# Splitting the first weights of a decoder trunk gate by gate, and loading x on one queue

## The chip, the core and the metric

The kernel runs on one core of a Trainium2 chip. The metric is the device time of one execution in microseconds. A core has a matrix engine (PE, with its weight loader PEld), a vector engine (DVE), a scalar engine (ACT), GpSimd (POOL) and a queue engine (SP) that here only issues loads and stores. Each engine works through its own list of instructions in order and waits on semaphores for the others. PE adds into PSUM accumulators; the other engines work on SBUF and read PSUM.

## The reference

A trunk of two layers over 256 tokens of width 1024, with float32 input and output. Each layer is a SwiGLU half-step, an attention (dilated windows in the first layer, selected blocks in the second) and another SwiGLU half-step. Cut to what the change touches, the first half-step:

```python
def rmsnorm(x, g):
    xf = x.astype(jnp.float32)
    y = xf * lax.rsqrt(jnp.mean(xf * xf, axis=-1, keepdims=True) + RMS_EPS)
    return (y * g.astype(jnp.float32)).astype(x.dtype)

def swiglu(h, w_gate, w_up, w_down):
    return (jax.nn.silu(h @ w_gate) * (h @ w_up)) @ w_down
```

with `w_gate` and `w_up` of 1024 x 2816. There are four such half-steps in the kernel; two in each layer, ahead of its attention and behind it.

## The kernel before

x is held transposed: 1024 features in eight blocks of 128 rows ("row blocks", k = 0 to 7), 256 tokens each, in one SBUF tile with the norms' gains, `gains_hT`. The 2816 features of an FFN are 22 blocks of 128 ("feature blocks", f). A gate or up sum of a feature block is a product over the eight row blocks of weights.

Products keep float32's accuracy by splitting each operand into a high part, which PE can take, and a low part, the rest. For weights ACT makes the high (`wh`, a copy with rounding) and DVE the low (`wl`, the difference). For x `parts_of` does the same with the gain as factor (L100 on ACT, L98 on DVE). `products_t` then runs, for a list of accumulators, first high weights against both parts of x (L201, 512 columns wide), for all accumulators, and then low weights against x's high (L207, 256 columns wide). Lists of `sums` give the order of the accumulators.

The norm's division by the root mean square is applied later, to the finished sums; `two_squares(k)` makes the squares of the row blocks k and k + 1 on ACT (L249) and adds them up on DVE.

The first FFN opens with `opening()`: its first four feature blocks, eight sums in eight PSUM accumulators, are computed row block by row block, so that PE can begin with the first 128 rows of weights. For each k it loads 512 columns of gate and 512 of up (the tile `raw`, gate and up side by side), calls `first(k)`, which loads x two row blocks at a time on SP and scales them, then `split`, which makes highs and lows, and then `step`, which emits PE's products. k = 0 is cut in two: columns 0 to 255 (feature blocks 0 and 1), whose weights ACT's own DMA queue loads at the program's start (L118 to L120), and columns 256 to 511 (feature blocks 2 and 3), which SP loads (L541). `split(raw, 0, slice(0, S), 1)` makes gate's and up's highs of the first half apart (`by=1`); the second half has one high over both (`by=2`) and each call has one low over both. x's row block 0 comes first on SP's queue, row block 1 third on ACT's queue (L121, `load_x`). `split` ends the step's work of ACT and DVE; `two_squares` follows from k = 4 on.

After the last row block `early_joined` copies and adds the two halves of each accumulator (ACT L414, DVE L415), which gives accumulators back to the feature blocks behind.

Who comes first on an engine is decided by a scheduler that takes instructions by priority and by a model of when their operands are ready; the order of the code is the priority. `queued(p)` holds the instructions emitted under it behind the instruction stored in `marks[p]`; this sets the order of issue and adds no wait. Behind the opening, `unit` loads and splits weights 1024 columns at a time (L169, L178, L179), and the down weights come as `right` and `made` pieces (L639, L667).

Of the kernel before, what the change touches and what calls it, by code (L numbers as in the profile page):

```python
# [10 lines left out]
F32 = mybir.dt.float32  # L11
F32R = mybir.dt.float32r
AF = mybir.ActivationFunctionType
# [3 lines left out]
S = 256  # L17
NT = S // P
D = 1024
KD = D // P  # L20
# [48 lines left out]
def trunk(ctx: ExitStack, tc: tile.TileContext, a: dict, out: bass.AP):  # L69
    nc = tc.nc  # L70
# [13 lines left out]
    def atile(shape, dt=F32, name="a"):  # L84
        return ap_.tile(shape, dt, tag="a", name=name)
# [7 lines left out]
    def parts_of(hi, lo, src, scale=1.0, later=None):  # L93

        def rest():
            if isinstance(scale, float):
                return first, nc.vector.tensor_sub(lo, src, hi.bitcast(F32))  # L97
            return first, nc.vector.scalar_tensor_tensor(lo, src, scale, hi.bitcast(F32), op0=ALU.mult, op1=ALU.subtract)  # L98

        first = nc.scalar.activation(hi, src, AF.Copy, scale=scale)  # L100
        (later or (lambda call: call()))(rest)
        return first
# [9 lines left out]
    gT, hT = both[:, :GX], both[:, GX:].rearrange("p (k s) -> p k s", s=S)  # L112

    def load_x(engine, k, end):
        cols = slice(GX + k * S if k else 0, GX + end * S)
        engine.dma_start(both[:, cols], a["gains_xT"][:, cols])

    early = rawp.tile([P, 2, 2, 512], F32, tag="raw", name="raw_0")  # L118
    for i, n in enumerate(("gate", "up")):
        nc.scalar.dma_start(early[:, 0, i, :S], a[f"ffn1_w_{n}"][0][:P, :S])  # L120
    load_x(nc.scalar, 1, 2)  # L121
    BF16 = mybir.dt.bfloat16
    fill = nc.const_aps.tensor(1.0, [P, 512], BF16)
    busy = trt("busy")
# [30 lines left out]
    marks, loads = {}, []  # L155

    def queued(p):

        stack = ExitStack()
        for ins in marks.get(p, ()):  # L160
            stack.enter_context(tc.issue_after(ins.ins))
        return stack
# [33 lines left out]
    def products_t(acs, wss, xs, first, last, between=None):  # L196


        for ac, ws in zip(acs, wss):
            for i, ((wh, wl), x) in enumerate(zip(ws, xs)):  # L200
                nc.tensor.matmul(ac, wh, flat(x), start=first and i == 0, stop=False)  # L201
            if between is not None:
                between()
                between = None
        for ac, ws in zip(acs, wss):
            for i, ((wh, wl), x) in enumerate(zip(ws, xs)):
                nc.tensor.matmul(ac[:, :S], wl, x[:, 0, :], start=False, stop=last and i == len(ws) - 1)  # L207
# [4 lines left out]
    def gain(k, gi, name, tag="x"):  # L212
        if tag == "x":
            if k % 2 == 0:
                twos[name] = xp.tile([P, 2, 2, S], F32R, tag=f"xx{k // 2}", name=f"x_{name}_{k}")
            x = twos[name][:, k % 2]
        else:
            x = xp.tile([P, 2, S], F32R, tag=f"{tag}{k}", name=f"x_{name}_{k}")
        g = gT[:, gi * KD + k:gi * KD + k + 1]
        parts_of(x[:, 0, :], x[:, 1, :], hT[:, k, :], g)  # L220
        return x

    def by_token(xs):
# [3 lines left out]
    class Norm:  # L227
# [11 lines left out]
        def scale(self, k):  # L239
            self.x.append(gain(k, self.gi, self.name))  # L240
# [5 lines left out]
        def two_squares(self, k):  # L246

            sq = atile([P, 2, S], name=f"sq_{self.name}_{k}")
            nc.scalar.activation(sq, hT[:, k:k + 2, :], AF.Square)  # L249
            if k:  # L250
                nc.vector.tensor_add(self.two, self.two, sq)
            else:
                self.two = sq
            if k == KD - 2:
                self.ss = sp.tile([P, S], F32, tag="ss", name=f"ss_{self.name}", bufs=1)
                nc.vector.tensor_add(self.ss, self.two[:, 0], self.two[:, 1])
# [173 lines left out]
    def ffn_blocks(name, wg, wu, norm, first=None, beside=(), sums=None, queue=()):  # L430
# [80 lines left out]
        def early_joined(f, acs):  # L511
            return (f, *acs, *[joined(ac, f"{name}_{n}{f}", atile([P, 2, S], name=f"j_{name}_{n}{f}")[:, 0])
                               for n, ac in zip("gu", acs)])

        def opening():

            acs = [[(trt if 2 * i + j < 3 else acc)(f"{name}_{n}{i}") for j, n in enumerate("gu")] for i in range(4)]
            parts = []

            def split(raw, k, cols=slice(0, 512), by=2):  # L520
                wh, wl = parts[k]
                for i in range(0, 2, by):
                    nc.scalar.activation(wh[:, i:i + by, cols], raw[:, i:i + by, cols], AF.Copy)
                nc.vector.tensor_sub(wl[:, :, cols], raw[:, :, cols], wh[:, :, cols].bitcast(F32))

            def step(fs, *ks):
                sums = [(i, n) for i in fs for n in range(2)]
                wss = [[(wh[:, n, i * P:(i + 1) * P], wl[:, n, i * P:(i + 1) * P]) for wh, wl in parts[ks[0]:ks[-1] + 1]]
                       for i, n in sums]
                products_t([acs[i][n] for i, n in sums], wss, norm.x[ks[0]:ks[-1] + 1], ks[0] == 0, ks[-1] == KD - 1,  # L530
                           norm.gather if fs[0] == 3 else None)

            for k in range(KD):
                if k % 2 == 0:
                    raws = rawp.tile([P, 2, 2, 512], F32, tag="raw", name=f"raw_{k}") if k else early
                raw = raws[:, k % 2]
                parts.append([wp.tile([P, 2, 512], F32R, tag=tag, name=f"{tag}_0_{k}") for tag in ("wh", "wl")])
                first(k)
                if k == 0:
                    for i, w in enumerate((wg, wu)):  # L540
                        nc.sync.dma_start(raw[:, i, S:], w[:P, S:512])  # L541
                    split(raw, 0, slice(0, S), 1)
                    split(raw, 0, slice(S, 512))
                else:
                    for i, w in enumerate((wg, wu)):
                        nc.sync.dma_start(raw[:, i], w[k * P:(k + 1) * P, :512])
                    split(raw, k, by=1 if k == 1 else 2)
                if k >= KD // 2:
                    norm.two_squares(2 * k - KD)
                    if k == KD - 1:  # L550
                        norm.fold()
                if k == 0:
                    step((0, 1), k)
                    step((2, 3), k)
                elif k < KD - 2:
                    step(range(4), k)
            for i in range(4):
                step((i,), KD - 2, KD - 1)
                done.append(early_joined(i, acs[i]))

        if first is not None:
            opening()
        for f in range(4 if first is not None else 0, KF, 2):
            ws = [weights(f, n) for n in "gu"]
            if f == 0:
                acs = [[(trt if i and n == "u" else acc)(f"{name}_{n}{i}") for n in "gu"] for i in range(2)]
                for k, pair in enumerate(zip(*ws)):
                    for i in range(2):
                        for ac, (wh, wl) in zip(acs[i], pair):
                            cols = slice(i * P, (i + 1) * P)  # L570
# [23 lines left out]
    def left_sums(pairs, homes):  # L594

        sums, halves = {}, []
        assert len(pairs) <= len(homes)
        for i, home in zip(pairs, homes):
            if home in ("wh", "wl"):
                parts = wp.tile([P, 2, 512], F32R, tag=home, name=f"left_{i}")  # L600
                sums[i] = (parts[:, 0], parts[:, 1])
            elif home in ("mk", "gf"):
                parts = xp.tile([P, 2, 512], F32R, tag=home, name=f"left_{i}")
                sums[i] = (parts[:, 0], parts[:, 1])
            elif home == "qk":
                if not halves:
                    both = ap_.tile([P, 2, 2, 512], F32R, tag=home, name=f"left_{i}", bufs=2)
                    halves += [both[:, 0], both[:, 1]]
                parts = halves.pop(0)
                sums[i] = (parts[:, 0], parts[:, 1])  # L610
            elif home == "pT":
                sums[i] = tuple(pp.tile([P, 512], F32R, tag=home, name=f"left_{i}_{j}") for j in range(2))
            else:
                sums[i] = tuple(xp.tile([P, 512], F32R, tag=f"{home[:2]}{int(home[2]) + j}", name=f"left_{i}_{j}")
                                for j in range(2))
        return sums
# [590 lines left out]
    def first(k):  # L1207
        if k % 2 == 0:
            load_x(nc.sync, k, k + 2 if k else 1)
        n0.scale(k)  # L1210
# [16 lines left out]
    w, n = a["a_w_qkv"][0], HG * DH  # L1227
# [42 lines left out]
    sums = left_sums(range(9), ("mk", "kx4", "kx6", "qk", "qk", "pT", "qk", "qk", "gf"))  # L1270
# [113 lines left out]
```

## Time and profile before

| | |
|---|---|
| median of three runs | 941.29 us (941.19, 941.29, 944.08) |
| the profiled execution | 941.45 us |
| its span, first to last instruction | 939.3 us |
| granted TensorE clock, mean | 0.998 |
| POOL busy | 196.8 us (21%) |
| data moved | 259.13 MB, 276 GB/s on average |

The span is what the trace covers; the remaining 2.15 us of the profiled execution lie around it. In the views below, L201 is line 201 of the kernel above, `f_g<-x_n,wh` names output and inputs, `128x512` their shape, and a bracket at a row's end is the time that the engine was idle ahead of it, with what ended that. `SPq` and `ACTq` rows are loads being issued. Buffer numbers are left out of names, so all four gate sums of the opening read `f_g`.

### The profile page before, as it was taken

The page shows a single profiled execution, that of the slowest core. Times are in us where ns is not written, and L with a number is a line of the kernel's source. Part 1 is how long each engine was busy: PE and PEld are TensorE (multiplying, and loading weights), DVE is VectorE, ACT ScalarE, POOL GpSimd, SP SyncE. Part 2 cuts the span into 40 slices and gives each one's busy share as a digit, 9 for nine tenths or more (in the row PEclk, how much of TensorE's full clock was granted, in tenths as well). Part 3 has the DMA queues.
Part 4 walks back from the last instruction along what each step waited for, and adds up shares of the span by engine and source line. Part 5 has one row for each costly group of instructions (what it writes and reads, how often), then busy time and mean ns, then how long its engine had stood idle before and what let it go on. Part 6 is the DMA issues. An engine that isn't in the chain of part 4 may idle for free.

```text
span 939.3 us, 15039 instructions
## 1 busy us (share of the span) xinstructions
PE 931.9 (99%) x5222; PEld 808.8 (86%) x5222; DVE 859.3 (91%) x1523; ACT 660.7 (70%) x1165; POOL 196.8 (21%) x211
## 2 busy tenths in 40 slices
PE   9999999999999999999999999999999999999997
PEld 7888888888899888888888888888888988888886
DVE  7999989988989999889989998899889889979887
ACT  7866667767887666667786656787587876657773
POOL 0132100024461401100024320000254623600000
PEclk9999999999999999999999999999999999999999
DMA  9999778988879999858999986799699689997791
GB/s 330 362 355 335 200 278 277 361 263 282 214 175 259 281 365 279 231 170 327 347 324 311 321 253 180 256 331 379 209 361 243 175 241 304 284 245 255 257 364 49
DMA packets 182380, 259.13 MB, mean 276 GB/s; under 512 B 28320, under 2 KB 126368, under 8 KB 178848
## 3 DMA queue, kind: packets, MB, share of 16 engines
q1 hardware_dynamic: 169504, 229.20, 73.3%
q0 software_dynamic: 12224, 28.32, 14.5%
q8 instruction: 41, 0.67, 0.3%
q10 hardware_dynamic: 576, 0.66, 0.2%
q14 instruction: 35, 0.29, 0.1%
HBM read 242.94 MB, written 48.76 MB: 311 GB/s over the span
## 4 chain that ended last, share of the span: by engine, by line
PE 99%; DMA 0%; ACT 0%; issue 0%; SPq 0%; POOLq 0%; DVE 0%; POOL 0%; ACTq 0%
PE f_g L201 17%; PE f_u L201 17%; PE f_u L207 9%; PE f_g L207 9%; PE dn_f_d L190 4%; PE dn_f_d L194 4%; PE dn_f_d L192 4%; PE dn_f_d_m L192 3%; PE dn_f_d_m L190 3%; PE dn_f_d_m L194 3%; PE ot_bo L887 1%; PE ot_ao L887 1%; PE ot_bo L888 1%; PE ot_ao L888 1%; PE ot_bo L889 1%; PE ot_ao L889 1%
## 5 line engine op out<-in xcount | busy, mean ns | idle before, releaser
L201 PE MATMUL f_g<-x_n,wh_f_g 128*128 128x512 f32 x672 | 170.4, 392 | 0.0
L201 PE MATMUL f_u<-x_n,wh_f_u 128*128 128x512 f32 x672 | 168.8, 390 | 0.0
L201 PEld LDWEIGHTS f_u<-x_n,wh_f_u 128*128 128x128 f32 x672 | 126.1, 188 | 26.6
L201 PEld LDWEIGHTS f_g<-x_n,wh_f_g 128*128 128x128 f32 x672 | 123.0, 188 | 23.7
L179 DVE TENSOR_TENSOR wl_f_u<-raw_f_u,wh_f_u 128x1024 fp32r<-128x1024 f32 x84 | 101.5, 1214 | 3.7 <-ACT wh_f_u L178 3.3
L178 ACT ACTIVATE wh_f_u<-raw_f_u 128x1024 fp32r<-128x1024 f32 x84 | 88.0, 1051 | 20.7 <-PE f_g L201 12.6
L179 DVE TENSOR_TENSOR wl_f_g<-raw_f_g,wh_f_g 128x1024 fp32r<-128x1024 f32 x84 | 101.6, 1214 | 0.8 <-ACT wh_f_g L178 0.5
L207 PE MATMUL f_u<-x_n,wl_f_u 128*128 128x256 f32 x672 | 96.7, 283 | 0.0
L207 PE MATMUL f_g<-x_n,wl_f_g 128*128 128x256 f32 x672 | 96.3, 282 | 0.0
L178 ACT ACTIVATE wh_f_g<-raw_f_g 128x1024 fp32r<-128x1024 f32 x84 | 87.0, 1051 | 11.6 <-PE f_u L201 6.4
L207 PEld LDWEIGHTS f_g<-x_n,wl_f_g 128*128 128x128 f32 x672 | 90.7, 191 | 4.0
L207 PEld LDWEIGHTS f_u<-x_n,wl_f_u 128*128 128x128 f32 x672 | 87.6, 192 | 0.0
L303 POOL TENSOR_TENSOR d_n<-w_n,expo 128x8 f32<-128x8 f32 x5 | 11.1, 2223 | 278.5 <-DVE w_n L299 278.5
L648 POOL COPY scrap<-act_f 128x1 f32<-128x1 f32 x19 | 41.3, 2176 | 129.5 <-ACT act_f L100 115.7
L677 POOL DMA_DIRECT2D made_f_d<-made_f_d x44 | 26.4, 643 | 95.4 <-DVE made_f_d L672 25.5
L100 ACT ACTIVATE left<-q_f 128x512 fp32r<-128x512 f32 x35 | 21.9, 626 | 29.8 <-DVE q_f L425 29.6
L980 POOL TENSOR_SCALAR sm_a<-sm_a,ls_a 128x128 f32<-128x128 f32 (+1 forms) x32 | 32.9, 1059 | 29.1 <-ACT sm_a L970 16.2
L480 ACT ACTIVATE g_f<-g_f 128x512 f32<-128x512 f32 x30 | 19.0, 632 | 27.9 <-DVE g_f L479 27.4
L980 POOL TENSOR_SCALAR sm_b<-sm_b,ls_b 128x128 f32<-128x128 f32 (+1 forms) x32 | 32.9, 1046 | 26.9 <-ACT sm_b L970 21.8
L97 DVE TENSOR_TENSOR left<-q_f,left 128x512 fp32r<-128x512 f32 x35 | 23.9, 683 | 14.0 <-ACT left L100 14.0
L100 ACT ACTIVATE act_f<-g_f 128x256 fp32r<-128x256 f32 x60 | 21.6, 407 | 13.3 <-DVE g_f L483 13.3
L414 ACT ACTIVATE u_f<-f_u 128x256 f32<-128x256 f32 x60 | 22.0, 384 | 12.4 <-PE f_u L207 12.3
(785 smaller groups left out, 2485.8 us busy)
## 6 DMA issues: line engine op xcount, KB each, us to landing
raw_f_g<-in_ffn_w_gate_dram SPq DMA_DIRECT2D x42, 1024.0 KB, 9.5
raw_f_u<-in_ffn_w_up_dram SPq DMA_DIRECT2D x42, 1024.0 KB, 8.1
raw_f_d<-in_ffn_w_down_dram SPq DMA_DIRECT2D x17, 1024.0 KB, 6.0
right_f_d<-in_ffn_w_down_dram SPq DMA_DIRECT2D x32, 512.0 KB, 9.9
raw_f_d<-in_ffn_w_down_dram SPq DMA_DIRECT2D x27, 512.0 KB, 4.8
made_f_d<-in_ffn_w_down_dram SPq DMA_DIRECT2D x44, 256.0 KB, 7.7
made_f_d<-made_f_d POOLq DMA_DIRECT2D x44, 256.0 KB, 6.6
right_f_d<-in_ffn_w_down_dram POOLq DMA_DIRECT2D x16, 512.0 KB, 8.6
```

The costliest lines, as they stand in the source:

```text
L97: return first, nc.vector.tensor_sub(lo, src, hi.bitcast(F32))
L100: first = nc.scalar.activation(hi, src, AF.Copy, scale=scale)
L178: nc.scalar.activation(wh, r, AF.Copy)
L179: nc.vector.tensor_sub(wl, r, wh.bitcast(F32))
L190: nc.tensor.matmul(ac, xh, wh, start=first, stop=False)
L192: nc.tensor.matmul(ac, xh, wl, start=False, stop=False)
L194: nc.tensor.matmul(ac, xl, wh, start=False, stop=last)
L201: nc.tensor.matmul(ac, wh, flat(x), start=first and i == 0, stop=False)
L207: nc.tensor.matmul(ac[:, :S], wl, x[:, 0, :], start=False, stop=last and i == len(ws) - 1)
L648: mark = nc.gpsimd.tensor_copy(scrap, latest[-1][:, 0, 0:1].bitcast(F32))
L677: nc.gpsimd.dma_start(self.home[:, j, n], part)
L980: done = nc.gpsimd.tensor_scalar(sm[:, seg], sm[:, seg], ls[:, t:t + 1], None, op0=ALU.mult)
```

## The change

Four edits, in `opening()`, the trunk's head, `gain` and `Norm.two_squares`.

- `load_x(nc.scalar, 1, 2)` goes from ACT's queue to SP's, as the fourth load there, behind the second halves of the first weights.
- `split` makes a high and a low for gate and one of each for up where `by=1`, which now holds for both halves of k = 0, for k = 1 and for k = 2; before, the low was always one over both.
- `step` lists the gate sums of its feature blocks ahead of the up sums; before they alternated.
- The first `two_squares` is emitted at k = 2, ahead of that step's split, and the others one step later; marks hold squares behind a scaled x or a high. The marks are set for every later norm too.

```diff
-    load_x(nc.scalar, 1, 2)
...
-        parts_of(x[:, 0, :], x[:, 1, :], hT[:, k, :], g)
+        marks["squares", 0 if k == 2 else -k] = [parts_of(x[:, 0, :], x[:, 1, :], hT[:, k, :], g)]
...
-            nc.scalar.activation(sq, hT[:, k:k + 2, :], AF.Square)
+            with queued(("squares", k)):
+                nc.scalar.activation(sq, hT[:, k:k + 2, :], AF.Square)
...
                 for i in range(0, 2, by):
-                    nc.scalar.activation(wh[:, i:i + by, cols], raw[:, i:i + by, cols], AF.Copy)
-                nc.vector.tensor_sub(wl[:, :, cols], raw[:, :, cols], wh[:, :, cols].bitcast(F32))
+                    own = slice(i, i + by)
+                    high = nc.scalar.activation(wh[:, own, cols], raw[:, own, cols], AF.Copy)
+                    marks["squares", 2 if k == 2 else -k] = [high]
+                    nc.vector.tensor_sub(wl[:, own, cols], raw[:, own, cols], wh[:, own, cols].bitcast(F32))
 
             def step(fs, *ks):
-                sums = [(i, n) for i in fs for n in range(2)]
+                sums = [(i, n) for n in range(2) for i in fs]
...
                         nc.sync.dma_start(raw[:, i, S:], w[:P, S:512])
+                    load_x(nc.sync, 1, 2)
                     split(raw, 0, slice(0, S), 1)
-                    split(raw, 0, slice(S, 512))
+                    split(raw, 0, slice(S, 512), 1)
                 else:
                     for i, w in enumerate((wg, wu)):
                         nc.sync.dma_start(raw[:, i], w[k * P:(k + 1) * P, :512])
-                    split(raw, k, by=1 if k == 1 else 2)
-                if k >= KD // 2:
+                    if k == 2:
+                        norm.two_squares(0)
+                    split(raw, k, by=1 if k < 3 else 2)
+                if k > KD // 2:
                     norm.two_squares(2 * k - KD)
```

ACT's first work on data, from x of row block 0 to the highs of k = 2, before (a name's last number is a buffer's; `wh_0` are highs of k = 0, `x_n_0` is x of row blocks 0 and 1):

```order
L100 ACTIVATE x_n_0_151<-gains_hT 128x256
L523 ACTIVATE wh_0_148<-raw_88 128x256 x2
L523 ACTIVATE wh_0_148<-raw_88 128x2x256
L100 ACTIVATE x_n_0_151<-gains_hT 128x256
L523 ACTIVATE wh_1_177<-raw_88 128x512 x2
L100 ACTIVATE x_n_2_206<-gains_hT 128x256 x2
L249 ACTIVATE sq_n_0_264<-gains_hT 128x512
L523 ACTIVATE wh_2_203<-raw_202 128x1024
```

and of the change:

```order
L100 ACTIVATE x_n_0_150<-gains_hT 128x256
L524 ACTIVATE wh_0_147<-raw_88 128x256 x4
L100 ACTIVATE x_n_0_150<-gains_hT 128x256
L524 ACTIVATE wh_1_180<-raw_88 128x512 x2
L100 ACTIVATE x_n_2_210<-gains_hT 128x256
L249 ACTIVATE sq_n_0_215<-gains_hT 128x512
L524 ACTIVATE wh_2_207<-raw_206 128x512
L100 ACTIVATE x_n_2_210<-gains_hT 128x256
L524 ACTIVATE wh_2_207<-raw_206 128x512
```

The wide high of k = 0 became two, that of k = 2 two with an x high between them, and the first square moved ahead of one x high.

PE's first half step (feature blocks 0 and 1 of k = 0; the accumulators are f_g and f_u of block 0, then of block 1), before:

```order
L201 MATMUL f_g_140<-x_n_0_151,wh_0_148 128x512
L201 MATMUL f_u_141<-x_n_0_151,wh_0_148 128x512
L201 MATMUL f_g_142<-x_n_0_151,wh_0_148 128x512
L201 MATMUL f_u_143<-x_n_0_151,wh_0_148 128x512
L207 MATMUL f_g_140<-x_n_0_151,wl_0_149 128x256
```

and of the change:

```order
L200 MATMUL f_g_139<-x_n_0_150,wh_0_147 128x512
L200 MATMUL f_g_141<-x_n_0_150,wh_0_147 128x512
L200 MATMUL f_u_140<-x_n_0_150,wh_0_147 128x512
L200 MATMUL f_u_142<-x_n_0_150,wh_0_147 128x512
L206 MATMUL f_g_139<-x_n_0_150,wl_0_148 128x256
```

Both gate sums now stand ahead of both up sums; every step of the opening is turned round in this way, and PE's list is otherwise as before.

ACT at the end of the opening, where the joins of feature blocks 0 and 1 meet the highs of feature blocks 4 and 5's weights, before:

```order
L178 ACTIVATE wh_f_g_0_404<-raw_f_g_402 128x1024
L178 ACTIVATE wh_f_g_4_408<-raw_f_g_402 128x1024
L414 ACTIVATE j_f_g_348<-f_g_140 128x256
L414 ACTIVATE j_f_u_351<-f_u_141 128x256
L178 ACTIVATE wh_f_u_0_414<-raw_f_u_412 128x1024
L414 ACTIVATE j_f_g_362<-f_g_142 128x256
L414 ACTIVATE j_f_u_365<-f_u_143 128x256
L178 ACTIVATE wh_f_u_4_418<-raw_f_u_412 128x1024
```

and of the change:

```order
L177 ACTIVATE wh_f_g_0_410<-raw_f_g_408 128x1024
L177 ACTIVATE wh_f_g_4_414<-raw_f_g_408 128x1024
L414 ACTIVATE j_f_g_354<-f_g_139 128x256
L414 ACTIVATE j_f_u_357<-f_u_140 128x256
L414 ACTIVATE j_f_g_368<-f_g_141 128x256
L414 ACTIVATE j_f_u_371<-f_u_142 128x256
L177 ACTIVATE wh_f_u_0_420<-raw_f_u_418 128x1024
L414 ACTIVATE j_f_g_382<-f_g_143 128x256
```

The joins of block 1 moved ahead of the first high of up's weights.

Elsewhere: SP's list has one load of up in layer 0's second FFN behind the four `made` copies that followed it, and a few neighbours of that kind exchanged in the first FFN; in the norms behind the two attentions the first square on ACT stands behind x highs, and the first highs of the weights stand behind two more x highs and a square. Nothing that is computed differs.

## Prediction

> **What bounds the kernel now.** First the page's busy times, then the waits of PE, then PE's timeline from the start.
>
> ```profile
> PE 931.9 (99%) x5222; PEld 808.8 (86%) x5222; DVE 859.3 (91%) x1523; ACT 660.7 (70%) x1165; POOL 196.8 (21%) x211
> ```
>
> PE is busy for 931.9 of 939.3 us. The list of PE's waits over the whole span has three rows (engine, line, what it waited for; total, times, longest):
>
> ```profile
> PE busy L126 <- PEq L1367: 0.8, 1, 0.8
> PE f_g L201 <- ACT wh L523: 0.4, 1, 0.4
> PE f_g L201 <- DVE x_n L98: 0.3, 1, 0.3
> ```
>
> So PE waits three times, 1.5 us in all, and the timeline puts all three before 6.70 us (start, duration, the wait in brackets):
>
> ```profile
> 4.70 0.47 PE L201 MATMUL f_g<-x_n,wh 128*128 128x512 f32 x1 [0.26 <-DVE x_n L98]
> ...
> 6.07 0.28 PE L207 MATMUL f_u<-x_n,wl 128*128 128x256 f32 x1
> 6.70 0.50 PE L201 MATMUL f_g<-x_n,wh 128*128 128x512 f32 x1 [0.35 <-ACT wh L523]
> ...
> 8.20 0.39 PE L201 MATMUL f_g<-x_n,wh 128*128 128x512 f32 x1
> 8.43 0.39 PE L201 MATMUL f_u<-x_n,wh 128*128 128x512 f32 x1
> ...
> 10.99 0.40 PE L201 MATMUL f_g<-x_n,wh 128*128 128x512 f32 x1
> ```
>
> 4.70 is the first product of row block 0 (k=0), 8.20 of k=1, 10.99 of k=2. Matmuls overlap, so starts count, not durations: 512-wide ones follow each other every 0.23 (8.20 to 8.43). A step is eight 512-wide and eight 256-wide matmuls. Step k=1 takes 10.99 − 8.20 = 2.79, step k=0 takes 8.20 − 4.70 = 3.50 for the same work. The difference, **0.71 us**, lies between its two halves: 6.07 to 6.70 is a wait for the highs of the second half's weights. That is the most this change can recover in the opening, and nothing behind it waits on PE: an edit elsewhere can only cost.
>
> **Why PE waits at 6.70.** ACT's and DVE's timelines, and the loads (issue time, time of issuing; then KB and us from issue to landing):
>
> ```profile
> 3.94 0.89 ACT L523 ACTIVATE wh<-raw 128x256 fp32r<-128x256 f32 x2
> 6.01 0.63 ACT L523 ACTIVATE wh<-raw 128x512 fp32r<-128x512 f32 x1 [1.19 <-DMA raw<-in_ffn_w_up_dram]
> 6.55 0.49 ACT L100 ACTIVATE x_n<-gains_hT 128x256 fp32r<-128x256 f32 x1
> 6.95 1.14 ACT L523 ACTIVATE wh<-raw 128x512 fp32r<-128x512 f32 x2
> ...
> 9.40 1.06 ACT L523 ACTIVATE wh<-raw 128x1024 fp32r<-128x1024 f32 x1
> ```
>
> ```profile
> 1.17 0.42 SPq L541 DMA_DIRECT2D raw<-in_ffn_w_gate_dram  x1
> 1.63 0.43 SPq L541 DMA_DIRECT2D raw<-in_ffn_w_up_dram  x1
> 1.65 0.45 ACTq L116 DMA_DIRECT2D gains_hT<-in_gains_xT_dram  x1
> 2.11 0.43 SPq L546 DMA_DIRECT2D raw<-in_ffn_w_gate_dram  x1
> 2.58 0.43 SPq L546 DMA_DIRECT2D raw<-in_ffn_w_up_dram  x1
> ...
> raw<-in_ffn_w_gate_dram SPq DMA_DIRECT2D x1, 128.0 KB, 3.0
> raw<-in_ffn_w_up_dram SPq DMA_DIRECT2D x1, 128.0 KB, 4.3
> gains_hT<-in_gains_xT_dram ACTq DMA_DIRECT2D x1, 128.0 KB, 4.5
> raw<-in_ffn_w_gate_dram SPq DMA_DIRECT2D x1, 256.0 KB, 4.5
> raw<-in_ffn_w_up_dram SPq DMA_DIRECT2D x1, 256.0 KB, 4.7
> ```
>
> The single high at 6.01 covers gate and up together. Gate's half landed at 1.17 + 3.0 = 4.2, up's at 1.63 + 4.3 = 5.9, so gate waits for up, and PE's next matmul reads gate.
>
> **The change, part by part.**
>
> *Gate and up split one by one, gate's sums first.* One 256-wide high takes:
>
> ```profile
> L523 ACT ACTIVATE wh<-raw 128x256 fp32r<-128x256 f32 x2 | 0.8, 408 | 0.1
> ```
>
> Gate's second half is then made behind the first two highs, at 3.94 + 0.89 = 4.83, and is ready at 5.24. PE wants it at 4.70 + 2.79/2 = 6.10: no wait. Up's second half starts at 6.01 as before, is ready at 6.42, and reaches PE some 0.06 later (the old high ended at 6.64, PE started at 6.70): 6.48. With the gate sums of both feature blocks ahead, up is wanted at 6.10 + 2 × 0.23 = 6.56. That holds by 0.08; beyond it PE stalls one for one. By the old order of sums it would be wanted at 6.33 and cost 0.15, so the reordering is worth having.
>
> The split costs ACT 2 × 0.41 − 0.63 = 0.19 for the second half of k=0, and as much or less for k=2 (k=1 was split already). DVE:
>
> ```profile
> 4.06 0.48 DVE L98 SCALAR_TENSOR_TENSOR x_n<-gains_hT,x_n 128x256 fp32r<-128x256 f32 x1 [3.17 <-ACT x_n L100]
> ...
> 6.68 0.69 DVE L524 TENSOR_TENSOR wl<-raw,wh 128x512 fp32r<-128x512 f32 x1 [1.13 <-ACT wh L523]
> ...
> L415 DVE TENSOR_TENSOR j_f_g<-f_g,j_f_g 128x256 f32<-128x256 f32 x4 | 1.7, 416 | 0.0
> ```
>
> A 256-wide low is not in the trace; another two-input operation of that size takes 0.42, so a split low costs about 2 × 0.42 − 0.69 = 0.14 more, four times (two in k=0, one each in k=1, k=2). The bounds are 0 and, if a 256-wide one took as long as the 512-wide, 0.69. All of this falls beside the idle 1.19 of ACT and 1.13 of DVE in the rows above; without that cover it would delay k=1 by 0.14 to 0.33.
>
> *x of the second row block on SP's queue.* It is issued at 2.11 instead of 1.65, ACT saves 0.45 of issuing, and each later SP load is issued 0.43 later, raw_1's gate at 2.58. Where x_1 lands the trace doesn't show. It landed at 1.65 + 4.5 = 6.13; in its new place the neighbour, raw_1's gate, landed at 2.11 + 4.5 = 6.64, an upper bound as that has twice the bytes. Taking those 256 KB off at the rate of the row below (0.71) gives 5.93 as the lower bound. I take 6.13, between them. Then ACT's high of x_1 follows up's, from 6.37 to 6.86, DVE's low from 6.89 to 7.37, and PE is released 0.16 later (4.06 + 0.48 = 4.54, PE at 4.70): **7.53**. Gate's high of k=1 runs 6.77 to 7.39 and reaches PE at 7.45. Back to back, k=1 would start at 4.70 + 2.79 = 7.49. So k=1 starts at about 7.5 instead of 8.20: **0.67 to 0.71** gained. The weights of k=2 are then wanted at 10.28. Their high began at 9.40 behind both x highs and, as the row shows, waited for nothing; a single one for gate (0.63) behind one x high fewer ends by 10.03.
>
> ```profile
> 3.00:4.00 1.00, 1.00 (x4) 0.30 (x3) 0.00 (x0) 0.99 (x4) 0.00 (x0) 1.00 1.08 347
> 7.00:8.00 1.00, 1.00 (x7) 0.83 (x6) 0.77 (x2) 1.00 (x4) 0.00 (x0) 1.00 1.06 371
> ```
>
> The last columns are the granted clock, DMA share and GB/s: the transfers run at 347 with two queues in use and at 371 with one. [...]
>
> *Squares moved, and what follows from it.* In the opening the square of blocks 0 and 1 goes between x_2 and its weights instead of behind both x. Later norms have their first square behind x highs and the weights' first high two places later. Those weights were ready long before use:
>
> ```profile
> 293.37 1.04 ACT L178 ACTIVATE wh_f_g<-raw_f_g 128x1024 fp32r<-128x1024 f32 x1
> ...
> 303.72 0.62 PE L201 MATMUL f_g<-x_n,wh_f_g 128*128 128x512 f32 x2
> ```
>
> Some 9 us lie between; two x highs of 0.49 and a square, like the 0.63 of another 512-wide operation of ACT, are 1.6 us. I cost this at nothing; without that cover it would be up to 1.6 at each norm.
>
> *One load of up moves behind four copies on SP* (layer 0's second FFN):
>
> ```profile
> 321.03 0.38 SPq L169 DMA_DIRECT2D raw_f_u<-in_ffn_w_up_dram  x1
> ...
> raw_f_u<-in_ffn_w_up_dram SPq DMA_DIRECT2D x1, 1024.0 KB, 10.2
> ...
> 351.81 3.79 PE L201 MATMUL f_u<-x_n,wh_f_u 128*128 128x512 f32 x16
> ```
>
> It landed at 331.2 and was used at 351.8. Four issues of 0.43 make it some 1.7 us later, more where one of them waits for its buffer. I cost this at nothing while the 20 us between, less the two highs of 1.06 and as much for the lows that split it, some 4, are not used up.
>
> *End of the opening.* What is late next:
>
> ```profile
> 24.74 1.06 ACT L178 ACTIVATE wh_f_u<-raw_f_u 128x1024 fp32r<-128x1024 f32 x1 [0.54 <-DMA raw_f_u<-in_ffn_w_up_dram]
> ...
> 27.31 0.41 DVE L415 TENSOR_TENSOR j_f_u<-f_u,j_f_u 128x256 f32<-128x256 f32 x1
> ...
> 28.00 2.00 PE L201 MATMUL f_g<-x_n,wh_f_g 128*128 128x512 f32 x8
> ```
>
> Feature block 4 writes an accumulator that this join gives back at 27.72, 0.28 ahead of PE. With PE 0.7 earlier the old order would stall by about 0.4. The new order puts both joins of block 1 ahead of the high at 24.74 that waits for its load, so they no longer stand behind that wait and its 1.06 us, and the 0.7 survives.
>
> **Sum.** The profiled execution took 941.45 (span 939.3 and 2.15 around it); less 0.70 gives 940.75. The median of the runs is 941.29, 0.16 lower, so by it 940.6. I forecast **940.7**, within 0.3% (2.8 us, about what a measurement of this kernel can tell from no change).
>
> **Rivals.** *x_1 late, gain halved:* x_1 lands at 6.64 like the load whose place it takes. Its high starts 0.08 later (as up's did), 0.49 + 0.48 + 0.16 follow, k=1 starts at 7.9: gain 0.3, 941.1. For it speaks the place in the queue, against it the bytes.
>
> *Slower, by the same load:* behind the weights x_1 decides the start of k=1, and from a landing later than about 6.95 on it starts later than 8.20. Were it to land at 2.58 + 4.7 = 7.28, k=1 would begin at 8.5 and the kernel take 941.8. Against it: that is the landing of a load with 384 KB more ahead of it or in it.
>
> *Nothing kept:* the opening gains 0.7, and a place without slack gives it back. The nearest is PE's weight loader late in the kernel:
>
> ```profile
> PEld dn_f_d_m L192 <- DVE wl_f_d_6c L739: 0.2, 1, 0.2
> ```
>
> Here DVE is just in time. But its work before that was itself released by PE, so it moves along; if not, 941.4. The same time comes out if up's load keeps PE waiting in the opening whatever the order.
>
> *A downstream stall of more than 2.8 us* from the reordered loads or splits: needs the 16 or 9 us above used up, and would give 944.3 or more.
>
> **Chances.** Forecast 0.76; x_1 late 0.11; nothing kept 0.06; slower by x_1 0.05; large stall 0.02. Range 940.2 to 941.9: below, the full 0.71 on the median (940.58) and a spread of 0.1 as between the two lower runs, with some room for x_0's high starting sooner without ACT's third issue; above, the slower rival. Faster by over 0.3% 0.01 (no 2.8 us to be had), same 0.96, slower 0.03 (the stall, or a run like the 944.08).
>
> **What would show it.** Right: k=1 starts near 7.5, PE's row of waits on ACT's highs at 6.70 is gone, block 4 starts near 27.3, and PE ends 0.7 sooner. Wrong: a wait on x_n's low ahead of k=1, a wait on up's high at 6.5, a wait at 27.3 for the joins, or any wait of PE behind 30 us.

## The result and the profile after

The change is slower: 949.48 us (median of 6 runs, 948.16 to 955.49) against 941.83 for the kernel before (6 runs, 941.19 to 944.08) on the same chip. The ratio is 1.0088 with a 95% interval of 1.0061 to 1.0114. The forecast of 940.7 and its range up to 941.9 were wrong. The profiled execution took 948.22 with a span of 946.1, so 6.8 us more span than before, at a granted clock of 0.995.

The page's busy times, after the change:

```profile
PE 935.5 (99%) x5222; PEld 811.0 (86%) x5222; DVE 859.4 (91%) x1527; ACT 659.0 (70%) x1167; POOL 191.8 (20%) x211
```

PE has the same 5222 matmuls and is busy 3.6 us longer. So about half of the 6.8 us is idle PE, and half is PE doing the same work more slowly. The waits of PE over the span (what it waited for; total, times, longest):

```profile
PE f_u L206 <- DVE wl_f_u L178: 3.8, 1, 3.8
PE busy L125 <- PEq L1372: 0.8, 1, 0.8
```

Both short waits of the opening are gone from the list, and one long wait is new: PE waits for lows of up's weights. PE's timeline shows the place; first after the change,

```profile
76.03 1.11 PE L206 MATMUL f_g<-x_n,wl_f_g 128*128 128x256 f32 x8
80.92 2.36 PE L206 MATMUL f_u<-x_n,wl_f_u 128*128 128x256 f32 x8 [3.78 <-DVE wl_f_u L178]
83.08 3.62 PE L200 MATMUL f_g<-x_n,wh_f_g 128*128 128x512 f32 x8
...
90.40 1.78 PE L200 MATMUL f_g<-x_n,wh_f_g 128*128 128x512 f32 x7
```

then the same products before:

```profile
76.18 1.11 PE L207 MATMUL f_g<-x_n,wl_f_g 128*128 128x256 f32 x8
77.14 1.12 PE L207 MATMUL f_u<-x_n,wl_f_u 128*128 128x256 f32 x8
...
83.66 2.00 PE L201 MATMUL f_g<-x_n,wh_f_g 128*128 128x512 f32 x8
```

These are feature blocks 12 to 14 of the first FFN; 83.66 is the start of block 14 before, 90.40 after. Up's lows were due 0.96 behind gate's (76.18 to 77.14), so at 76.99, and came at 80.92: **3.93 us** of standstill. From there to block 14 PE took 9.48 instead of 6.52: **2.96 us**, at half clock, as the next view shows. Less the 0.15 that PE was still ahead at 76.03, that makes 6.74: the whole loss in the span of this execution, one of the shortest of the six.

Stretches of 2 us, after the change (PE, PEld, DVE, ACT, POOL busy with counts; granted clock, DMA share, GB/s):

```profile
78.00:80.00 2.00, 0.00 (x0) 0.00 (x0) 0.69 (x2) 1.97 (x5) 0.44 (x1) 1.00 1.09 349
80.00:82.00 2.00, 1.07 (x4) 0.93 (x4) 2.00 (x3) 0.91 (x2) 1.12 (x1) 0.50 1.09 347
82.00:84.00 2.00, 2.00 (x8) 1.75 (x8) 2.00 (x6) 0.47 (x2) 0.61 (x2) 0.50 1.14 258
```

The clock stays at 0.50 until 86 us; before, it is 1.00 in all these stretches. Matmuls take nearly twice as long at 0.50 (3.62 for eight wide ones against 2.00).

**Back along the chain.** DVE and ACT, after the change:

```profile
79.31 0.43 DVE L97 TENSOR_TENSOR act_f<-act_f,act_f 128x256 fp32r<-128x256 f32 x1 [5.26 <-ACT act_f L100]
79.65 2.35 DVE L178 TENSOR_TENSOR wl_f_u<-raw_f_u,wh_f_u 128x1024 fp32r<-128x1024 f32 x2
```

```profile
67.94 1.06 ACT L177 ACTIVATE wh_f_u<-raw_f_u 128x1024 fp32r<-128x1024 f32 x1 [0.49 <-PE f_g L200]
...
76.70 1.06 ACT L177 ACTIVATE wh_f_g<-raw_f_g 128x1024 fp32r<-128x1024 f32 x1 [5.42 <-DMA raw_f_g<-in_ffn_w_gate_dram]
...
78.87 0.40 ACT L100 ACTIVATE act_f<-act_f 128x256 fp32r<-128x256 f32 x1
```

The lows that PE wants could have been made from 69 us on: their last high began at 67.94. They stand on DVE behind one low of an activation (`act_f` of block 10), which needs its high, which stands on ACT behind highs of blocks 14 and 15's gate weights, whose load has not landed. A load for a *later* pair of blocks stops PE, because three engines work their lists in order. Before, the same pair of lows began at 73.78:

```profile
73.78 2.35 DVE L179 TENSOR_TENSOR wl_f_u<-raw_f_u,wh_f_u 128x1024 fp32r<-128x1024 f32 x2
```

It ended at 76.13, only 1.0 us before PE took it up at 77.14. That was the slack of this place.

**Why the load is late.** The load with its landing time, before, then SP's own list and the transfers around it after the change (KB, us from issue to landing):

```profile
60.27 0.42 SPq L169 DMA_DIRECT2D raw_f_g<-in_ffn_w_gate_dram  x1
...
raw_f_g<-in_ffn_w_gate_dram SPq DMA_DIRECT2D x1, 1024.0 KB, 8.3
```

```profile
60.95 0.55 SPq L644 DMA_DIRECT2D right_f_d<-in_ffn_w_down_dram  x1
61.56 0.61 SPq L168 DMA_DIRECT2D raw_f_g<-in_ffn_w_gate_dram  x1
...
raw_f_g<-in_ffn_w_gate_dram SPq DMA_DIRECT2D x1, 1024.0 KB, 15.1
right_f_d<-in_ffn_w_down_dram POOLq DMA_DIRECT2D x1, 512.0 KB, 10.8
right_f_d<-in_ffn_w_down_dram SPq DMA_DIRECT2D x1, 512.0 KB, 10.5
```

The load is issued 1.3 us later but lands 8.1 us later (76.7 against 68.6). Beside it run two transfers of 512 KB into the `right` pieces of the down weights: the fourth and last copy, now issued by SP directly ahead of it (at 48.78 before, ahead of the third group of `made` loads), and the first of POOL's adding transfers, which add another part of the weights to a piece of the same tile. POOL paces those with a tiny copy that reads the newest activation:

```python
        def paced(self):
            scrap = sp.tile([P, 1], F32, tag="scrap", name="scrap")
            mark = nc.gpsimd.tensor_copy(scrap, latest[-1][:, 0, 0:1].bitcast(F32))
            with tc.issue_after(mark.ins):
                self.add()
```

POOL before, then after:

```profile
61.11 3.59 POOL L648 COPY scrap<-act_f 128x1 f32<-128x1 f32 x1 [5.04 <-ACT act_f L100]
64.65 1.16 POOL L644 DMA_DIRECT2D right_f_d<-in_ffn_w_down_dram  x1
```

```profile
59.68 0.87 POOL L653 COPY scrap<-act_f 128x1 f32<-128x1 f32 x1 [2.76 <-ACT act_f L100]
60.50 1.16 POOL L649 DMA_DIRECT2D right_f_d<-in_ffn_w_down_dram  x1
```

The pacing copy starts 1.4 us earlier and takes 2.7 less, so the adding transfer starts **4.15 us** earlier: beside the gate load instead of behind it. What released it earlier is ACT, before and after:

```profile
58.76 1.99 ACT L178 ACTIVATE wh_f_g<-raw_f_g 128x1024 fp32r<-128x1024 f32 x2
60.65 0.40 ACT L100 ACTIVATE act_f<-act_f 128x256 fp32r<-128x256 f32 x1
```

```profile
59.20 0.42 ACT L100 ACTIVATE act_f<-act_f 128x256 fp32r<-128x256 f32 x1 [0.72 <-DVE act_f L464]
...
60.05 1.04 ACT L177 ACTIVATE wh_f_g<-raw_f_g 128x1024 fp32r<-128x1024 f32 x1
```

The high of `act_f` of block 8 stands ahead of two highs of gate's weights (blocks 12 and 13) instead of behind them. Together, in 64 to 66 us, the transfers move 184 GB/s after the change against 357 before:

```profile
64.00:66.00 2.00, 2.00 (x15) 1.84 (x14) 2.00 (x4) 0.00 (x0) 0.19 (x1) 1.00 0.98 184
```

```profile
64.00:66.00 2.00, 2.00 (x14) 1.80 (x13) 2.00 (x6) 0.04 (x1) 2.00 (x3) 1.00 1.06 357
```

### The profile page after: what moved, and what is told of

Same layout as the page of the kernel before. It is cut to its first block, busy times and chain, and to the rows that moved or that the text cites. A ratio compares the mean times of both kernels' runs of the same rounds, so it can differ in the third digit from the quotient of the medians.

```text
span 946.1 us, 15060 instructions
## 1 busy us (share of the span) xinstructions
PE 935.5 (99%) x5222; PEld 811.0 (86%) x5222; DVE 859.4 (91%) x1527; ACT 659.0 (70%) x1167; POOL 191.8 (20%) x211
## 4 chain that ended last, share of the span: by engine, by line
PE 97%; DMA 2%; ACT 0%; DVE 0%; SPq 0%; issue 0%; POOLq 0%; POOL 0%
PE f_g L200 17%; PE f_u L200 16%; PE f_u L206 9%; PE f_g L206 9%; PE dn_f_d L189 4%; PE dn_f_d L191 4%; PE dn_f_d L193 4%; PE dn_f_d_m L191 3%; PE dn_f_d_m L189 3%; PE dn_f_d_m L193 3%; DMA raw_f_g<-in_ffn_w_gate_dram 2%; PE ot_ao L892 1%; PE ot_bo L892 1%; PE ot_bo L893 1%; PE ot_ao L893 1%; PE ot_ao L894 1%
## 5 line engine op out<-in xcount | busy, mean ns | idle before, releaser
L303 POOL TENSOR_TENSOR d_n<-w_n,expo 128x8 f32<-128x8 f32 x5 | 13.2, 2632 | 274.5 <-DVE w_n L299 274.4
L653 POOL COPY scrap<-act_f 128x1 f32<-128x1 f32 x19 | 36.0, 1894 | 134.6 <-ACT act_f L100 112.4
L100 ACT ACTIVATE x_n<-gains_hT 128x256 fp32r<-128x256 f32 x48 | 21.6, 498 | 12.5 <-DVE gains_hT L845 8.5
```

The costliest lines, as they stand in the source:

```text
L653: mark = nc.gpsimd.tensor_copy(scrap, latest[-1][:, 0, 0:1].bitcast(F32))
```

## The experiments

Eleven kernels, each timed against the kernel before on the same chip. Single runs of the kernel before lie between 941.1 and 948.3, so the intervals count, not single runs. Two exchanges are to be told apart: SP's fourth copy ("copy ahead" as before, "behind" as after the change) and POOL's first adding transfer ("late" at 64 to 65.5 us as before, "early" at 60 to 61).

### x alone, and the change without it

`x_alone` is the kernel before with only x of row block 1 moved:

```diff
-    load_x(nc.scalar, 1, 2)
...
                         nc.sync.dma_start(raw[:, i, S:], w[:P, S:512])
+                    load_x(nc.sync, 1, 2)
```

> Only x of the second row block is moved to SP's queue; split, sums and squares are as before. The order theory (one load more on SP's queue makes the scheduler put the fourth copy of right_f_d behind the third group of made_f_d, the gate load behind it lands some 8 us later, PE stops once for about 4 us near 77 us and then runs some 6 us at half clock) expects the same stop, and 947.5 to 949.5. The head-start theory (PE reaches the loads too early because the opening is shorter) expects no stop, since nothing in the opening is faster here: 941.0 to 942.5.

Measured: 948.79, ratio 1.0075 (1.0056 to 1.0093), adding transfer at 60.82. PE's waits:

```profile
PE f_u L206 <- DVE wl_f_u L178: 3.8, 2, 3.6
```

`x_on_act` is the change with these two lines put back.

> The whole change but for the move of x: x of the second row block stays third on ACT's queue. The order theory expects no stop of PE near 77 us, as SP's order in the first FFN is that of before, and 940.6 to 941.3; the first product of k=1 starts at 7.5 to 7.7 if what held it at 7.89 was gate's weights of k=1 landing at 7.18 behind x. The head-start theory, and a third one by which the split's own instructions cost the time, expect 947 or more.

Measured: 941.97, ratio 0.9999 (0.9988 to 1.0010), no stop in the first FFN, adding transfer at 64.34, the gate load landing 7.3 after its issue. So the loss comes with x's change of queue and is whole without the split, the order of sums or the squares. It doesn't come from where x lands: k = 1 began at 7.89 in the change and at 7.87 without x's move. It comes through what the scheduler makes of the move 50 us later.

### SP's fourth copy, from both sides

`copy_pinned` is the change with the third group of `made` loads held behind the fourth copy; only that copy changes its place.

```diff
+                if self is f10 and not self.copies:
+                    for n in range(4):
+                        tc.add_manual_dep(m10.last[2, n].ins, copy.ins.name, ...
```

> The whole change, and the fourth copy of right_f_d ahead of the third group of made_f_d on SP, as before; that one instruction of the kernel moves and no other. The order theory expects the gate load to land near 69 instead of 76.6, no stop of PE near 77 us, and 940.9 to 941.4. The head-start theory expects 947 or more.

Measured: 949.18, ratio 1.0060 (1.0041 to 1.0080). The adding transfer is still early (60.29), the gate load lands 10.8 after its issue, and the stop at 77 is gone; but another comes one pair later, behind a load of up (issued at 73.91, landing 12.8 later against 9.9 before):

```profile
PE f_g L206 <- DVE wl_f_g L178: 3.0, 1, 3.0
```

`copy_late` is the kernel before with the copy moved behind that group, and the gate load behind the copy.

```diff
...
-                with tc.issue_after(loads[-1].ins):
-                    nc.sync.dma_start(*self.copies.pop(0))
+                fourth = self is f10 and len(self.copies) == 1
+                with tc.issue_after((m10.last[2, 3] if fourth else loads[-1]).ins):
+                    copy = nc.sync.dma_start(*self.copies.pop(0))
...
```

> The kernel before, with the fourth copy of right_f_d put behind the third group of made_f_d on SP and nothing of the change. The order theory expects a stop of PE of 3 to 5 us near 77 us and 946 to 950. If the other loads that the change moved in the first FFN (one gate load ahead of the first group of made_f_d) are needed for it too: 941.3 to 943. The head-start theory: 941.3.

Measured: 942.82, ratio 1.0018 (1.0000 to 1.0037), from 941.27 to 949.78; adding transfer at 65.17. The profiled run, 947.96, is the second longest of ten and has two stops at 88.0 to 90.8:

```profile
PE f_g L209 <- DVE wl_f_g L181: 2.1, 2, 1.3
```

The theory until here, that the copy's place decides, falls: put back it saves nothing that can be told, moved alone it costs about 0.2%, at the edge of what these runs can tell.

### SP's whole order, from both sides

An SP order of the first FFN is forced by edges along a list (g, u: loads of gate and up by feature block; r: copies; m: `made` groups):

```diff
+    for one, two in zip(order, order[1:]):
+        tc.add_manual_dep(two.ins, one.ins.name, ...
```

`sp_as_before` is the change with SP's order of before, "g4 u4 g6 u6 r0 g8 u8 r1 m0 g10 u10 r2 m1 g12 u12 r3 m2 g14 u14 ...".

> The whole change, with SP's loads of the first FFN held in the order of before (the fourth gate load behind the first group of made_f_d, the fourth copy of right_f_d ahead of the third group). The theory that SP's order makes the stop expects no stop of PE behind 70 us and 940.9 to 941.8. If the other engines' order in the first FFN, which the move of x changed too, makes it, the time stays at 945 to 949.

Measured: 952.05, ratio 1.0102 (1.0061 to 1.0142): not better than the change itself, with the adding transfer at 60.79. `sp_as_after` is the kernel before with SP's order of the change, "... r1 g10 m0 u10 r2 m1 g12 u12 m2 r3 g14 ...".

> The kernel before, opening and all, with SP's loads of the first FFN held in the order of the changed kernel. The theory of SP's order expects a stop of PE of 3 to 4 us near 77 us and 946 to 950. The other engines' order, or the head start, as the cause: 941.3 to 943.

Measured: 944.66, ratio 1.0021 (1.0001 to 1.0040), with the adding transfer at 65.48 and no stop in the profiled run. So SP's list is worth about 0.2%, and the rest of the 0.9% is elsewhere.

### The adding transfer, and DVE's order

`add_later` is the change with POOL's first two adding transfers one step later:

```diff
-... [(at, f10) for at in (4, 5, 7, 8)])
+... [(at, f10) for at in (5, 6, 7, 8)])
```

> The whole change, with POOL's first two adding transfers of right_f_d one step of the first FFN later each. If the fourth copy of right_f_d and the gate load behind it are slow because they run beside POOL's adding transfer (2048-byte packets of 140 to 340 ns on both queues between 60 and 70 us, 186 GB/s in all), the gate load lands by 72 instead of 76.6 and the stop at 77 us is gone or under 1 us: 941 to 945. If only the place behind the third group of made_f_d counts, the load still lands near 76 and the time stays at 947 to 949.5.

Measured: 944.22, ratio 1.0026 (1.0001 to 1.0052), the first adding transfer at 78.06, no stop at 77, the gate load landing 10.2 after its issue. About two thirds of the loss are gone (by the interval, two fifths at least), with the change's order untouched on SP and on ACT. The single runs go from 940.92 to 950.89, and three of the ten are longer than 947.5, so the loss does not go in every run.

`lows_first` is the change with DVE's low of block 10's activation behind the two lows that PE waits for:

```diff
+            if name == "f10_u12":
+                tc.add_manual_dep(marks["low", "f10", 10].ins, low.ins.name, ...
```

> The whole change, with one instruction of DVE moved: the low of the eleventh activation block (act_f) goes behind the two up lows of the pair that PE waits for. If PE stops at 77 us because those lows stand behind that act_f, which waits for ACT, which waits for the next pair's gate load, then the stop at 77 us goes though the gate load still lands near 76.6, and the time falls to 941 to 945 (a later stop of the same kind may stay). If PE waits for the load itself: 947 to 949.5.

Measured: 950.32, ratio 1.0073 (1.0048 to 1.0097). The stop at 77 is gone though the gate load lands at 77.6, so the chain through DVE's list was read rightly. But PE then waits for what comes behind:

```profile
PE f_u L202 <- ACT wh_f_u L177: 1.5, 1, 1.5
PE f_g L208 <- DVE wl_f_g L178: 1.1, 1, 1.1
```

The transfers stay late, and another engine's list passes that on to PE.

### ACT's one high, from both sides

`high_back` is the change with the high of block 8's activation held behind the two gate highs, as before. SP's fourth copy goes back to its old place by itself, through the scheduler.

```diff
+    tc.add_manual_dep(marks["act", "f10", 8].ins, marks["wh", "f10_g12", 4].ins.name, ...
```

> The whole change, with one instruction of ACT held in its old place: the high of the ninth activation block of the first FFN (act_f) behind the two gate highs of the seventh pair instead of ahead of them. POOL's pacing copy reads that high, and POOL's first adding transfer of right_f_d follows it. The new theory (the high comes early, the copy falls where DVE is idle and takes 0.9 us instead of 3.6, the adding transfer starts at 60.5 instead of 64.6 and runs beside SP's copy of right_f_d, both slow, and the gate load behind lands late) expects the transfer at 64 to 65, the gate load by 72, no stop of PE near 77 us, and 940.9 to 942.5. If the early transfer is only a sign of something else that the move of x did: 946 to 951.

Measured: 943.25, ratio 1.0018 (1.0001 to 1.0035). POOL is back at its old pace, and the gate load lands 7.6 after its issue:

```profile
62.27 3.26 POOL L653 COPY scrap<-act_f 128x1 f32<-128x1 f32 x1 [5.33 <-ACT act_f L100]
65.47 1.16 POOL L649 DMA_DIRECT2D right_f_d<-in_ffn_w_down_dram  x1
```

`high_ahead` is the kernel before, opening and all, with that one high ahead of the two gate highs. SP's fourth copy moves behind by itself.

```diff
+    tc.add_manual_dep(marks["wh", "f10_g12", 0].ins, marks["act", "f10", 8].ins.name, ...
```

> The kernel before, opening and x as before, with that one high of ACT put ahead of the two gate highs, where the change has it. The new theory expects the adding transfer at 60 to 61.5, the gate load at 74 or later, a stop of PE near 77 us, and 946 to 951, with nothing of the change in it. Otherwise: 941.3 to 944.

Measured: 947.51, ratio 1.0066 (1.0053 to 1.0079). The gate load lands at 74.0, as the theory had it. In the profiled run, 944.91 and the shortest of the six, PE stops several times from 77 us on for 1.0 us at most, not once for 4, and the clock stays at 1.00 there. POOL's rows and PE's waits in it:

```profile
60.68 0.47 POOL L648 COPY scrap<-act_f 128x1 f32<-128x1 f32 x1 [4.16 <-ACT act_f L100]
61.09 1.16 POOL L644 DMA_DIRECT2D right_f_d<-in_ffn_w_down_dram  x1
```

```profile
PE f_u L207 <- DVE wl_f_u L179: 1.1, 3, 0.4
PE f_g L207 <- DVE wl_f_g L179: 1.0, 1, 1.0
```

This pair settles the place: one order of ACT, 17 us ahead of the stop, turns most of the loss on without any of the change's edits and off with all of them. It doesn't settle what that order does by itself, since SP's copy moves along with it. For that the table of all kernels is read by columns (medians in us):

| | copy ahead | copy behind |
|---|---|---|
| adding transfer late | before 941.8 to 942.2, `x_on_act` 942.0, `high_back` 943.3 | `copy_late` 942.8, `sp_as_after` 944.7 |
| adding transfer early | `copy_pinned` 949.2, `sp_as_before` 952.1 | change 949.5, `x_alone` 948.8, `high_ahead` 947.5, `lows_first` 950.3 |

Each kernel of the lower row is slower by its median than each of the upper, by 2.8 us where they are nearest (947.5 against 944.7); between the columns there is no such line. `add_later` (944.2), which takes the transfer out of the stretch altogether, belongs to the upper row. It is the one kernel that parts the transfer from ACT's order, which it has as the change has it (the high of block 8 at 60.03, ahead of the two gate highs). So the early adding transfer carries most of the loss. By the ratios the line is thinner: the intervals of `copy_pinned` (from 1.0041) and `add_later` (up to 1.0052) overlap.

How the early transfer reaches PE is shown for the change alone. Where PE stops, and how often, differs among the lower row's kernels, and the landing of the gate load does not sort them: it landed at 71.7 in `copy_pinned` and at 71.9 in `add_later`, whose profiled runs took 949.55 and 943.18.

### A try at a faster kernel

`act_add_later` is `x_on_act` with the adds of `add_later`.

> The change without the move of x, and POOL's first two adding transfers one step later each: a try at a faster kernel. If the stretch from 56 to 95 us keeps its slack, what the opening gains (0.3 to 0.7) is kept in every run: 940.5 to 941.3, against 941.97 for the same kernel with the transfers in their old steps. If the transfers then crowd the loads of the pairs behind: 942 to 946.

Measured: 944.53, ratio 1.0021 (1.0004 to 1.0038): no faster. Its first adding transfer starts at 72.70, so it too belongs with the upper row. The profiled run has no stop between 30 and 130 us; its waits lie in several other places, of 0.2 to 0.5 us each, one of them at the start of feature block 4 (28.09), and their cause stays open. No kernel here beat the one before.

## Why the prediction was wrong

- **"... an edit elsewhere can only cost."** True, and that cost should have been priced. The prediction named one load that moves on SP in layer 0's second FFN and gave it 20 us of cover. The exchanges in the first FFN, which the order of instructions also showed, got no price at all: SP's were named without one, and ACT's high of block 8 was not named. This is the step that failed: the row of before needed for it (lows done at 76.13, taken up at 77.14) was in the trace, with 1.0 us of slack.
- **The change's reach.** Of x's move the prediction counted the issues on SP and ACT in the opening. Its larger effect was on the scheduler's order far behind: one ACT high, through POOL's pacing copy, the start of a transfer, a load and DVE. Why the scheduler exchanges those two on ACT when x changes its queue was not traced.
- **Rival "a downstream stall of more than 2.8 us".** The right outcome ("944.3 or more"), with a chance of 0.02 and the wrong places: it needed "the 16 or 9 us above used up". Neither was touched. Nor did it hold that a stall costs more than its length; here 3.93 us cost 2.96 more through the clock.
- **Rival "nothing kept".** Its mechanism, a place without slack, was right in kind. "The nearest" was not PE's weight loader late in the kernel, and the price was not the 0.7 us gained, since more than the opening's lead had moved.
- **The opening's 0.67 to 0.71.** The mechanism holds: the waits of the opening are gone from PE's list. The size was off. k = 1 starts at 7.89, 0.31 sooner, not 0.67, and no run shows the 0.70 of the sum. PE, then the loads of x_1 and of gate's k = 1, then ACT, all after the change:

```profile
7.89 1.20 PE L200 MATMUL f_g<-x_n,wh 128*128 128x512 f32 x4
```

```profile
gains_hT<-in_gains_xT_dram SPq DMA_DIRECT2D x1, 128.0 KB, 4.4
raw<-in_ffn_w_gate_dram SPq DMA_DIRECT2D x1, 256.0 KB, 4.6
```

```profile
7.21 1.28 ACT L524 ACTIVATE wh<-raw 128x512 fp32r<-128x512 f32 x2 [0.21 <-DMA raw<-in_ffn_w_gate_dram]
```

The sum put x_1 at 6.13 and gate's high of k = 1 at 6.77, behind x_1's. x_1 landed at 2.11 + 4.4 = 6.5, so the x_1-late rival was nearer there. But gate's weights came last: issued at 2.58, as the prediction itself said, they landed at 7.18, and ACT waited for them. The sum moved their issue by 0.43 and left their landing where it was, at 6.64. They explain only the last part of the delay: PE's last product of k = 0 began at 7.55, and low products follow each other every 0.12, so about 0.2 us. `x_on_act` was expected to begin k = 1 at 7.5 to 7.7 with these weights out of the way and began it at 7.87, with no gap ahead of it; there its first two products lay 0.56 apart (4.70 to 5.26; 0.30 before), 0.49 in the change (4.53 to 5.02). Why was not traced. The lead was 0.19 at k = 2 and 0.14 at feature block 4 (27.86 against 28.00); that part was not traced further. And an opening doesn't start k = 1 at a fixed time: in the profiled runs it began between 7.74 and 8.77 with the change's opening, between 8.20 and 8.55 with that of before. A lead of 0.3 us is smaller than this scatter, and `x_on_act`, which had 0.34 at feature block 4 in its profiled run, shows none in its time (0.9999).
- **Rival "slower, by the same load".** x_1 would have had to land later than about 6.95; it landed at 6.5. The sign was right, the mechanism not.
- **The range.** Its upper end, 941.9, was set by events in the opening alone. A place with 1.0 us of slack behind loads that change their order has no such narrow bound.

## What to carry to other kernels

When a kernel's list is made by a scheduler, an edit's cost is not where the edit is: compare the order of every engine over the whole program, and for each exchange compute, from rows of before, how far ahead of its use the thing behind it was ready. A transfer that is paced by a tiny instruction starts when that instruction gets its turn, so an order of another engine decides which loads it runs beside (here it started 4.15 us sooner, beside the gate load instead of behind it). And where the bounding engine has about 1 us of slack, price a stop at its length plus what the clock does after it (here 3.93 and 2.96 us).

## What the runs showed of the hardware

**The clock after a stop.** Behind the stop of 3.93 us the granted clock was 0.50 for about 6 us and cost 2.96 more. It fell after shorter stops too; `copy_pinned`, with its stop of 3.0 us (87.6 to 90.6):

```profile
88.00:90.00 2.00, 0.00 (x0) 0.00 (x0) 1.59 (x3) 1.64 (x5) 0.00 (x0) 0.91 0.66 224
90.00:92.00 2.00, 1.22 (x4) 0.93 (x4) 2.00 (x4) 0.06 (x1) 0.00 (x0) 0.50 0.15 17
```

Behind the two stops of `copy_late`, 2.1 us in all, the clock fell too. It was 0.50 from 92 to 96. PE was busy 0.73 and 1.17 of 2 us ahead of that; in `lows_first` it was busy as little, 0.74 and 1.17, and kept 1.00. First `copy_late`, then `lows_first`:

```profile
88.00:90.00 2.00, 0.73 (x4) 0.53 (x4) 2.00 (x4) 1.15 (x4) 0.00 (x0) 1.00 1.01 355
90.00:92.00 2.00, 1.17 (x5) 0.97 (x5) 2.00 (x3) 1.33 (x2) 0.00 (x0) 0.66 0.58 146
```

```profile
90.00:92.00 2.00, 0.74 (x4) 0.53 (x4) 2.00 (x3) 0.42 (x2) 0.54 (x1) 1.00 0.87 319
92.00:94.00 2.00, 1.17 (x7) 0.96 (x8) 2.00 (x4) 0.19 (x1) 0.00 (x0) 1.00 0.96 289
```

So a stop of 3.0 us was enough for the clock to fall, and in `copy_late` two of 2.1 us in all; in `lows_first` stops of 1.1, 0.7 and 0.4 us (89.9 to 93.6), 2.2 in all, were not. Why two like stretches ended unlike, no run here shows.

**Two transfers into one kind of tile.** SP's copy and POOL's adding transfer, 512 KB each and side by side, took 10.5 and 10.8 us, while all transfers together moved 184 GB/s instead of 357 at a DMA share that was as high (0.98 against 1.06). So the DMA engines were as busy with half the bytes. Their times alone say little: apart from each other the copy took 11.7 (at 48.78 before) and 7.3 (in `copy_late`), the adding transfer 9.4 (before). But the traces have the traffic beside each of them alone. The adding transfer without the copy, from the kernel before:

```profile
70.00:72.00 2.00, 2.00 (x16) 1.88 (x15) 2.00 (x5) 2.00 (x4) 0.00 (x0) 1.00 1.10 231
```

The copy without the adding transfer, from `copy_late`:

```profile
62.00:64.00 2.00, 2.00 (x11) 1.63 (x10) 2.00 (x3) 1.34 (x2) 2.00 (x1) 1.00 0.65 178
```

The adding is dear by itself: in that stretch of the kernel before POOL's queue took 82% of the DMA engines' time and moved 0.31 of 0.46 MB. With the copy the traffic is lower still, but at a share of 0.65, so there the DMA engines stood partly idle. `high_ahead` has 167 GB/s at 62 to 64 us at a share of 0.70, with no packet of POOL's queue in the stretch yet: that is the copy too. Why the copy alone cost so little time (`copy_late`, 1.0018) and the early adding so much more is not shown.

**The pacing copy.** One element for each partition took 3.59 us before, 0.87 after and 0.47 in `high_ahead`. Before, it started beside one of DVE's lows of 1024 columns and ended only behind the next two (61.71 to 64.06); after, it ended with the low beside which it had started (59.29 to 60.51). That DVE's lows held the copy up is the author's reading of these times; no run isolates it, and POOL's spans are rough. The expectation of `high_back` puts the early copy where DVE is idle; in the change DVE was busy beside all of it (59.29 to 60.84). The copy's length matters here because the kernel before owes the late start of its adding transfer in good part to it: of the 4.15 us, 2.7 are the copy's.
